# Both products of an encoder's MLP by one level of Strassen's algorithm, in its form with seven products and shared sums

## The chip, the cores and the metric

The kernel runs on one core of one Trainium2 chip, in one launch. The metric is the device time of one execution in microseconds; the kernel before takes 1821.32 us, the median of three runs (1820.94, 1821.32 and 1827.15). On this scale a difference of 0.5%, some 9 us, is about what a comparison can tell from none.

## The reference

One encoder layer runs over 1024 prompt frames and 64 sample frames, together 1088 tokens, with a width of 1024. Four mixers (a convolution, two kinds of attention, a linear recurrence) and a memory attention come first. The change is in the last part, a squared-ReLU MLP with 4096 inner columns, and the final norm:

```
h = _rmsnorm(x, norm_ffn[l])
return x + jnp.square(jax.nn.relu(h @ w_up[l])) @ w_down[l]      # w_up (1024, 4096), w_down (4096, 1024)
...
y_prompt = _rmsnorm(x, norm_final)
```

All inputs and outputs are fp32. Every product is made to nearly fp32 accuracy out of rounded parts: each operand is split into a high part and a low part, and three matmuls (high by high, high by low, low by high) are added in PSUM.

## The kernel before, in words

Everything is held transposed: the partitions are 128 of the 1024 channels, the columns are tokens. Tokens are in two groups, group 0 with 512 and group 1 with 576, the latter cut into chunks of 320 and 256 columns (`GR`, line 207), since one matmul writes at most one bank of 512 columns. The residual `xT[g][k]` stays in SBUF from the output projection to the end.

`load_w` (line 179) fetches a weight block of 128 output columns into one of two `wr` buffers, and `split` (line 166) makes its two parts: ScalarE copies to the rounded type, VectorE subtracts. `mm3` (line 185) does three matmuls for each of the kt blocks of 128 in the sum. Every matmul carries its own weight load.

The MLP (lines 1181 to 1266) goes through the 4096 inner columns in 8 steps `c` of 512. In each step `up` makes 4 blocks of 128 inner rows, for both groups: 24 matmuls for each chunk, then Relu and Square on ScalarE, and a split into the pair `hid`. Then `down` takes, for each of the 8 output blocks `m`, a weight block of 512 by 128, 12 matmuls for each chunk, and one VectorE addition of the PSUM sum to `xT` (line 1240). In the first step the whole of group 0 comes ahead of group 1, because the norm of group 1 needs the last sums of the memory attention's output projection (`dense_add`, line 1051). In the last step `down` goes chunk by chunk, and after each chunk `finish` transposes it on TensorE, makes the final norm and stores it (lines 1199 to 1224).

`rms_stats` (line 1030) sums the squares of a group over its 8 blocks, lets TensorE add over partitions, and takes the inverse root (`rstd_chain`, line 140); `rms_apply` (line 1040) multiplies and splits.

A planner at build time fixes each engine's order of instructions: it takes what its model holds ready by priority, which is the order of the program unless `tc.cur_priority` says otherwise, and gives out the buffers of a pool as earlier users let go of them. On the chip every engine goes through its list in that order. All large transfers of this part are issued on SP's queue.

## Time and profile before

| | |
|---|---|
| median of three runs | 1821.32 us |
| the profiled execution's own time | 1827.22 us |
| its span in the trace | 1825.5 us |
| granted TensorE clock, mean over the span | 0.988 |
| TensorE (PE) busy | 1766.5 us (97%) |
| VectorE (DVE) busy | 1056.7 us (58%) |
| ScalarE (ACT) busy | 802.6 us (44%) |
| GpSimd (POOL) busy | 98.4 us (5%) |
| moved by DMA | 141.79 MB |

A busy share is an average over stages with different limits: the mixers fill the first 800 us or so, the MLP everything from 1045 us to the end. Matmuls are pipelined and their recorded durations overlap, so the time that one takes up is read from start to start. DVE records overlap a little too.

### The profile page before, as it was taken

What the parts mean: (1) busy time and instruction counts of PE and PEld (TensorE: products, weight loads), DVE (VectorE), ACT (ScalarE), POOL (GpSimd) and SP (SyncE); (2) the same over time, 40 slices, a digit from 0 to 9 for tenths busy, and PEclk for the clock granted to TensorE, in tenths of its full rate; (3) what the DMA queues carried; (4) which work ended last, traced back from release to release, by engine and by line L of the source; (5) the groups of instructions that cost most, each with busy time, mean ns of one, the idle gap of its engine ahead of it and who ended that gap; (6) DMA issues with size and microseconds to landing.
All of it is one profiled execution on the core that took longest, in us unless ns stands there. A gap on an engine that the chain in (4) does not pass through costs nothing. (4 is left out here: it accounts for less than half of the span.)

```text
span 1825.5 us, 29328 instructions
## 1 busy us (share of the span) xinstructions
PE 1766.5 (97%) x11454; PEld 1542.6 (85%) x11467; DVE 1056.7 (58%) x2209; ACT 802.6 (44%) x1691; POOL 98.4 (5%) x199
## 2 busy tenths in 40 slices
PE   7999999999999998999999999999999999999997
PEld 5877767777877886988899999999999999999987
DVE  6455779879887887857768564232323232332335
ACT  6464566455447843546455361413131323232233
POOL 3011202001120200000000000000000000000000
PEclk9999999999999999999999999999999999999999
DMA  8221222222223565422322322111111112111212
GB/s 252 75 73 41 60 53 77 59 80 71 82 77 103 152 179 163 140 87 65 109 76 70 107 73 58 35 52 42 44 44 47 47 36 58 35 52 36 58 41 99
DMA packets 225178, 141.79 MB, mean 78 GB/s; under 512 B 14478, under 2 KB 214607, under 8 KB 225039
## 3 DMA queue, kind: packets, MB, share of 16 engines
q1 hardware_dynamic: 224783, 139.90, 25.8%
q8 instruction: 90, 1.47, 0.3%
q14 instruction: 49, 0.40, 0.1%
q0 software_dynamic: 256, 0.01, 0.0%
HBM read 111.97 MB, written 27.87 MB: 77 GB/s over the span
## 5 line engine op out<-in xcount | busy, mean ns | idle before, releaser
L71 PE MATMUL pu<-ap,wh 128*128 128x512 f32 (+2 forms) x1536 | 363.9, 328 | 0.1
L74 ACT ACTIVATE wh<-wr 128x1024 fp32r<-128x1024 f32 (+1 forms) x196 | 170.2, 868 | 428.5 <-PE pdn L71 285.9
L71 PEld LDWEIGHTS pu<-ap,wh 128*128 128x128 f32 x1536 | 261.7, 189 | 20.7 <-DVE ap L168 0.3
L71 PE MATMUL pu<-ap,wl 128*128 128x320 f32 (+2 forms) x768 | 251.1, 327 | 0.0
L168 DVE TENSOR_TENSOR wl<-wr,wh 128x1024 fp32r<-128x1024 f32 (+1 forms) x196 | 193.3, 986 | 91.8 <-ACT wh L74 85.7
L1240 DVE TENSOR_TENSOR xT<-xT,pdn 128x512 f32<-128x512 f32 (+2 forms) x192 | 102.2, 532 | 202.8 <-PE pdn L71 202.8
L71 PE MATMUL pa<-ap,wh 128*128 128x256 f32 (+2 forms) x768 | 189.2, 335 | 7.8 <-ACT ap L74 6.8
L71 PE MATMUL pm<-hx,wh 128*128 128x512 f32 (+1 forms) x640 | 180.2, 369 | 1.3 <-DVE hx L276 0.8
L71 PE MATMUL pdn<-aq,wh 128*128 128x256 f32 (+1 forms) x896 | 181.2, 295 | 0.0
L71 PE MATMUL pm<-ap,wh 128*128 128x256 f32 (+1 forms) x768 | 165.0, 308 | 0.0
L71 PEld LDWEIGHTS pu<-ap,wl 128*128 128x128 f32 x768 | 145.3, 189 | 10.2
L71 PEld LDWEIGHTS pdn<-aq,wh 128*128 128x128 f32 x896 | 148.4, 189 | 4.4
L71 PEld LDWEIGHTS pa<-ap,wh 128*128 128x128 f32 x768 | 133.7, 194 | 19.1 <-ACT ap L74 7.8
L71 PE MATMUL pdn<-hid,wh 128*128 128x512 f32 x448 | 139.3, 392 | 0.0
L71 PE MATMUL pdn<-aq,wl 128*128 128x320 f32 x448 | 132.6, 296 | 0.0
L71 PEld LDWEIGHTS pm<-hx,wh 128*128 128x128 f32 x640 | 112.1, 194 | 21.2 <-issue 1.7
L71 PE MATMUL pa<-ap,wl 128*128 128x512 f32 (+2 forms) x384 | 128.7, 336 | 1.3 <-DVE wl L168 1.3
L71 PEld LDWEIGHTS pm<-ap,wh 128*128 128x128 f32 x768 | 124.2, 192 | 5.1 <-issue 1.9
L760 DVE SCALAR_TENSOR_TENSOR y<-ext,cwT,y 128x288 f32<-128x288 f32 (+2 forms) x300 | 125.3, 446 | 2.9
L71 PE MATMUL pm<-ap,wl 128*128 128x256 f32 (+1 forms) x384 | 114.3, 298 | 0.0
L71 PE MATMUL pm<-hx,wl 128*128 128x512 f32 (+1 forms) x320 | 113.4, 354 | 0.0
L74 ACT ACTIVATE rl<-pu 128x320 f32<-128x320 f32 (+2 forms) x96 | 44.8, 467 | 150.4 <-PE pu L71 150.4
(335 smaller groups left out, 3120.2 us busy)
## 6 DMA issues: line engine op xcount, KB each, us to landing
wr<-in_w_up_dram SPq DMA_DIRECT2D x36, 512.0 KB
wr<-in_w_down_dram SPq DMA_DIRECT2D x64, 256.0 KB
wr<-in_w_in_dram SPq DMA_DIRECT2D x24, 512.0 KB
wr<-in_w_out_dram SPq DMA_DIRECT2D x16, 512.0 KB
wr<-in_w_mq_dram SPq DMA_DIRECT2D x16, 512.0 KB
wr<-in_w_mo_dram SPq DMA_DIRECT2D x32, 256.0 KB
xt<-in_x_prompt_dram SPq DMA_DIRECT2D x8, 512.0 KB
wr<-in_w_mk_dram SPq DMA_DIRECT2D x8, 512.0 KB
```

The lines of the kernel that those rows point to most:

```text
L71: nc.tensor.matmul(out, lhsT=lhsT, rhs=rhs, start=start, stop=stop, **kw)
L74: nc.scalar.activation(out=out, in_=in_, func=func, **kw)
L168: V.tensor_tensor(out=lo, in0=src, in1=hi.bitcast(F32), op=ALU.subtract)
L760: V.scalar_tensor_tensor(out=y[:, :n], in0=ext[:, j:j + n], scalar=cwT[:, ct, j:j + 1], in1=y[:, :n], op0=ALU.mult, op1=ALU.add)
L1240: V.tensor_tensor(out=xs, in0=xs, in1=ps[:, :cn], op=ALU.add)
```

## The change

Both products are cut into two by two blocks. For the product up, a unit is a pair of adjacent blocks of 128 output rows; the other cut halves the sum (channels 0 to 511 and 512 to 1023), and the third cut takes the token groups as halves, 512 and 576, where the shorter one counts as padded with zeros. A unit has 7 products in place of 8: B11, B21 and T4 with 512 columns, T1, T2, B22 and T3 with 576, each with half the sum (`mul`, 12 matmuls for each piece). The 576 columns go as pieces of 288 into two banks (`mul2`). The operands are sums: T1 to T4 of the normed inputs are built and split once ahead of the loop; sums of the weight blocks (`sums`, four additions of 512 columns) and five splits (`wform`) are made for each of the 16 units. Products are added partly in PSUM and partly by VectorE (`plus`), with one shared intermediate `t1`. Relu and Square come after the sums. Then GpSimd forms the T1 to T4 of the inner activations, and seven stores for each unit write them to `hid_d` in DRAM. The residual is stored to `x2_d` as the memory attention's second half finishes it, and loaded again ahead of the product down.

The product down has 8 steps `c`, each reading 14 tiles of `hid_d` and splitting them (`hidden`; for T3 and T4 the subtraction is on GpSimd), and for each of 4 pairs `j` of output blocks 7 products with 6 matmuls for each piece, 7 weight splits of 256 columns, four weight sums on GpSimd, and the additions to `xT`. The shared term is gathered in `a1[j]` by GpSimd. In the last step two of the seven products are done after the others, by token chunks, so that `finish` can follow each. The old code for the MLP (lines 1181 to 1266) is gone; its `finish` returns nearly unchanged.

```
+    x2_d = dram.tile([KD, P, T], F32, name="x2_d")
+    hid_d = dram.tile([DFF // (2 * P), 7, P, 576], F32, name="hid_d")
...
+    UB = {"ap": 16, "aq": 12, "xt": 20}
+    up_ = ctx.enter_context(tc.tile_pool(name="up", bufs=16))
+    pools.append(up_)
+    def unit(tag, dt=F32):
+        return up_.tile([P, 576], dt, name=tag, tag=tag, bufs=UB[tag])
+    xT = [[unit("xt")[:, :n] for k in range(KD)] for g, (t0, n, _) in enumerate(GR)]
...
+            rstd_chain(up_, cn, ps[:, :cn], [("xt", UB["xt"])] * 3, scale=1.0 / D, out=rr[:, c0:c0 + cn])
...
+    def normed(g, k, gains, rr, c0, cn):
+        hf = unit("xt")
+        V.scalar_tensor_tensor(out=hf[:, :cn], in0=xT[g][k][:, c0:c0 + cn], scalar=gains[:, k:k + 1],
+                               in1=rr[:, c0:c0 + cn], op0=ALU.mult, op1=ALU.mult)
+        return hf
...
+            if store:
+                nc.sync.dma_start(out=x2_d[m][:, t0:t0 + n], in_=xT[g][m])
...
+                rr0, h3 = rr, rms_apply(0, g_ffn, rr, 0)
+            dense_add(g, w_mo, HALF * P, KD - HALF, om[HALF:], ps1, store=True)
...
+    N1, N2, HN = 512, 576, 288
+    NU = DFF // (2 * P)
+    B11, T1, B21, T2, B22, T3, T4 = range(7)
+    WIDTH = {B11: N1, B21: N1, T4: N1, T1: N2, T2: N2, B22: N2, T3: N2}
...
+    def bank():
+        return psm.tile([P, 512], F32, name="pw", tag="w", bufs=2)
+    def banks():
+        return psm.tile([P, 2, 512], F32, name="pz", tag="z", bufs=3)
...
+    def mul(ps, w, b, start, cols):
+        for k, (bh, bl) in enumerate(b):
+            last = k == len(b) - 1
+            mm(ps, w[0][:, k], bh[:, cols], start and k == 0, False, skip_group_check=not start)
+            mm(ps, w[0][:, k], bl[:, cols], False, False, skip_group_check=not start)
+            mm(ps, w[1][:, k], bh[:, cols], False, last, skip_group_check=not start)
+    def mul2(ps, w, b, start, n=N2):
+        mul(ps[:, 0, :HN], w, b, start, slice(0, HN))
+        mul(ps[:, 1, :n - HN], w, b, start, slice(HN, n))
+    def split_pool(hi, lo, src):
+        act(hi, src, AF.Copy)
+        Q.tensor_tensor(out=lo, in0=src, in1=hi.bitcast(F32), op=ALU.subtract)
...
+    t1s = [fz.tile([P, N2], F32, name=f"t1_{i}", bufs=1) for i in range(2)]
+    for t in t1s:
+        Q.memset(t[:, N1:], 0.0)
+    rr1 = rms_stats(1, psm, "w")
+    late = [lambda: fz.tile([P, N2], F32R, name="fz", tag="fz")] * 12
+    late = [lambda: unit("aq", F32R)] * 12 + late
+    hb = {B11: h3[:4], B21: h3[4:]}
+    for f in (T2, T1, B22):
+        hb[f] = [[late.pop(0)() for _ in range(2)] for k in range(4)]
+    for f in (T3, T4):
+        hb[f] = [[unit("xt", F32R) for _ in range(2)] for k in range(4)]
+    for k in range(4):
+        h12 = normed(1, k, g_ffn, rr1, 0, N2)
+        h11 = normed(0, k, g_ffn, rr0, 0, N1)
+        V.tensor_tensor(out=h11[:, :N1], in0=h12[:, :N1], in1=h11[:, :N1], op=ALU.subtract)
+        act(h11[:, N1:], h12[:, N1:], AF.Copy)
+        h22 = normed(1, k + 4, g_ffn, rr1, 0, N2)
+        t2 = unit("xt")
+        V.tensor_tensor(out=t2, in0=h22, in1=h11, op=ALU.subtract)
+        split(*hb[T2][k], t2)
+        split(*hb[T1][k], h11)
+        split(*hb[B22][k], h22)
+        Q.tensor_tensor(out=h12, in0=h22, in1=h12, op=ALU.subtract)
+        split_pool(*hb[T3][k], h12)
+        h21 = normed(0, k + 4, g_ffn, rr0, 0, N1)
+        Q.tensor_tensor(out=h21[:, :N1], in0=h21[:, :N1], in1=t2[:, :N1], op=ALU.subtract)
+        split_pool(hb[T4][k][0][:, :N1], hb[T4][k][1][:, :N1], h21[:, :N1])
...
+    def wform(src):
+        pr = [unit("ap", F32R)[:, :4 * P].rearrange("p (k c) -> p k c", k=4) for _ in range(2)]
+        split(*pr, src)
+        return pr
+    def sums(a11, a12, a21, a22, s1, eng):
+        eng.tensor_tensor(out=s1, in0=a21, in1=a22, op=ALU.add)
+        eng.tensor_tensor(out=a21, in0=a11, in1=a21, op=ALU.subtract)
+        eng.tensor_tensor(out=a11, in0=s1, in1=a11, op=ALU.subtract)
+        eng.tensor_tensor(out=a12, in0=a12, in1=a11, op=ALU.subtract)
+    def square(c):
+        act(c, c, AF.Relu)
+        act(c, c, AF.Square)
+    def plus(out, a, b, eng=V):
+        eng.tensor_tensor(out=out, in0=a, in1=b, op=ALU.add)
+    for i in range(NU):
+        r1 = fetch_w(w_up, 0, KD, 2 * i * P)
+        r2 = fetch_w(w_up, 0, KD, (2 * i + 1) * P)
+        wh, wl = (wp.tile([P, KD, P], F32R, name=nm, tag=nm) for nm in ("wh", "wl"))
+        split(wh, wl, r1)
+        s1 = unit("ap")[:, :4 * P].rearrange("p (k c) -> p k c", k=4)
+        sums(r1[:, :4], r1[:, 4:], r2[:, :4], r2[:, 4:], s1, V)
+        S2, S1, S4, S3, A22 = (wform(r) for r in (r1[:, :4], s1, r1[:, 4:], r2[:, :4], r2[:, 4:]))
+        t1 = t1s[i % 2]
+        W, Z, X = bank(), banks(), banks()
+        mul(W, (wh[:, :4], wl[:, :4]), hb[B11], True, slice(0, N1))
+        act(t1[:, :N1], W, AF.Copy)
+        mul2(Z, S2, hb[T2], True)
+        c12 = unit("ap")
+        plus(halves(c12), halves(t1), Z[:, :, :HN])
+        mul2(X, S1, hb[T1], True)
+        c22 = unit("ap")
+        plus(halves(c22), halves(t1), X[:, :, :HN])
+        mul(W, (wh[:, 4:], wl[:, 4:]), hb[B21], False, slice(0, N1))
+        c11 = unit("ap")
+        act(c11[:, :N1], W, AF.Relu)
+        act(c11[:, :N1], c11[:, :N1], AF.Square)
+        mul2(X, S4, hb[B22], False)
+        plus(halves(c12), halves(c12), X[:, :, :HN])
+        square(c12)
+        mul2(Z, S3, hb[T3], False)
+        plus(halves(c22), halves(c22), Z[:, :, :HN])
+        square(c22)
+        mul2(Z, A22, hb[T4], False, N1)
+        c21 = unit("ap")
+        plus(c21[:, :HN], t1[:, :HN], Z[:, 0, :HN])
+        plus(c21[:, HN:N1], t1[:, HN:N1], Z[:, 1, :N1 - HN])
+        square(c21[:, :N1])
...
+        t3, t2, t4 = (unit("xt") for _ in range(3))
+        Q.tensor_tensor(out=t3, in0=c22, in1=c12, op=ALU.subtract)
+        Q.tensor_tensor(out=c12[:, :N1], in0=c12[:, :N1], in1=c11[:, :N1], op=ALU.subtract)
+        Q.tensor_tensor(out=t2, in0=c22, in1=c12, op=ALU.subtract)
+        Q.tensor_tensor(out=t4[:, :N1], in0=c21[:, :N1], in1=t2[:, :N1], op=ALU.subtract)
+        for f, t in ((B11, c11), (T1, c12), (B21, c21), (T2, t2), (B22, c22), (T3, t3), (T4, t4)):
+            nc.sync.dma_start(out=hid_d[i, f, :, :WIDTH[f]], in_=t[:, :WIDTH[f]])
+    fz_ctx.close()
...
+    places = ([lambda: pools[0].tile([P, 576], F32R, name="ap", tag="ap")] * 16
+              + [lambda: fq.tile([P, 576], F32R, name="fq", tag="fq")] * 6
+              + [lambda: unit("ap", F32R)] * 14 + [lambda: unit("aq", F32R)] * 8)
+    turn = [0]
+    def place():
+        turn[0] += 1
+        return places[(turn[0] - 1) % len(places)]()
...
+    def hidden(c):
+        hb = {}
+        for f in (B11, T1, B21, T2, B22, T3, T4):
+            hb[f] = []
+            n = WIDTH[f]
+            for i in (2 * c, 2 * c + 1):
+                raw = unit("aq")[:, :n]
+                nc.sync.dma_start(out=raw, in_=hid_d[i, f, :, :n])
+                pr = [place()[:, :n] for _ in range(2)]
+                (split_pool if f in (T3, T4) else split)(*pr, raw)
+                hb[f].append(pr)
+        return hb
...
+    def down_w(c, j):
+        raw = wp.tile([P, KD, P], F32, name="wr", tag="wr").rearrange("p (k m) c -> p k m c", m=2)
+        nc.sync.dma_start(out=raw.rearrange("p k m c -> p k (m c)"),
+                          in_=w_down[4 * c * P:4 * (c + 1) * P, 2 * j * P:2 * (j + 1) * P].rearrange(
+                              "(k p) c -> p k c", p=P))
+        raw = raw.rearrange("p (k h) m c -> p h m k c", h=2)
+        return [raw[:, h, m] for m in range(2) for h in range(2)]
...
+    NC = DFF // (4 * P)
+    for c in range(NC):
+        hb = hidden(c)
+        end = c == NC - 1
+        if end:
+            for i in range(2):
+                gf.append(unit("ap"))
+                nc.sync.dma_start(out=gf[i][:, :512], in_=norm_final[i * 512:(i + 1) * 512].partition_broadcast(P))
+        for j in range(NJ):
+            x11, x21 = xT[0][2 * j], xT[0][2 * j + 1]
+            x12, x22 = xT[1][2 * j], xT[1][2 * j + 1]
+            a11, a12, a21, a22 = down_w(c, j)
+            p1, p2 = wpair(), wpair()
+            A11, A12 = form(p1, 0, a11), form(p1, 2, a12)
+            s1 = fs.tile([P, 2, P], F32, name="s1", tag="s1")
+            sums(a11, a12, a21, a22, s1, Q)
+            if not end:
+                S1, S4 = form(p1, 4, s1), form(p2, 4, a12)
+            S2, S3, A22 = form(p2, 0, a11), form(p2, 2, a21), form(p2, 6, a22)
+            W, Z = bank(), banks()
+            mul(W, A11, hb[B11], True, slice(0, N1))
+            if c:
+                tmp = unit("aq")[:, :N1]
+                act(tmp, W, AF.Copy)
+                plus(a1[j], a1[j], tmp, Q)
             else:
+                act(a1[j], W, AF.Copy)
+            if not end:
+                X = banks()
+                mul2(X, S1, hb[T1], True)
+                plus(halves(x22), halves(x22), X[:, :, :HN])
+            mul(W, A12, hb[B21], False, slice(0, N1))
+            plus(x11, x11, W)
+            mul2(Z, S2, hb[T2], True)
+            plus(halves(x12), halves(x12), Z[:, :, :HN])
+            if not end:
+                mul2(X, S4, hb[B22], False)
+                plus(halves(x12), halves(x12), X[:, :, :HN])
+            mul2(Z, S3, hb[T3], False)
+            plus(halves(x22), halves(x22), Z[:, :, :HN])
+            mul2(Z, A22, hb[T4], False, N1)
+            plus(x21[:, :HN], x21[:, :HN], Z[:, 0, :HN])
+            plus(x21[:, HN:], x21[:, HN:], Z[:, 1, :N1 - HN])
+            if end:
+                plus(x21, x21, a1[j])
+                plus(x12[:, :N1], x12[:, :N1], a1[j], Q)
+                plus(x22[:, :N1], x22[:, :N1], a1[j], Q)
+        if end:
+            ws = []
+            for j in range(NJ):
+                a11, a12, a21, a22 = down_w(c, j)
+                p = wpair()
+                s1 = fs.tile([P, 2, P], F32, name="s1", tag="s1")
+                sums(a11, a12, a21, a22, s1, Q)
+                ws.append((form(p, 0, s1), form(p, 2, a12)))
+            finish(0, 0, N1)
+            for c0, cn in GR[1][2]:
+                cols = slice(c0, c0 + cn)
+                for j in range(NJ):
+                    x12, x22 = xT[1][2 * j][:, cols], xT[1][2 * j + 1][:, cols]
+                    W = bank()[:, :cn]
+                    mul(W, ws[j][0], hb[T1], True, cols)
+                    plus(x22, x22, W)
+                    mul(W, ws[j][1], hb[B22], False, cols)
+                    plus(x12, x12, W)
+                finish(1, c0, cn)
```

## Rows read from the trace of the kernel before

**Rows 1.** The page, busy time by engine, and its chain of waits by engine and line.
```profile
PE 1766.5 (97%) x11454; PEld 1542.6 (85%) x11467; DVE 1056.7 (58%) x2209; ACT 802.6 (44%) x1691; POOL 98.4 (5%) x199
...
PE 40%; ACT 0%; DVE 0%; issue 0%; DVEq 0%
```
**Rows 2.** The chain of waits in order of time: start us, us, what.
```profile
1142.07 47.44 PE pu L71 x288
1189.51 47.52 PE pdn L71 x288
```
**Rows 3.** Windows: stretch and length; PE, PEld, DVE, ACT, POOL busy; PEclk; DMA share; GB/s.
```profile
300.00:600.00 300.00, 289.32 (x2058) 234.89 (x2068) 251.34 (x564) 162.10 (x369) 32.55 (x45) 0.97 0.27 79
900.00:1000.00 100.00, 99.37 (x714) 94.39 (x714) 71.51 (x176) 55.88 (x139) 0.00 (x0) 1.00 0.27 81
...
0.00:90.00 90.00, 77.20 (x475) 63.07 (x476) 52.83 (x122) 50.59 (x116) 21.50 (x74) 1.00 0.55 164
```
**Rows 4.** Timeline of PE in the MLP: start us, us, instruction; three matmuls for each pair.
```profile
1071.45 0.46 PE L71 MATMUL pu<-ap,wh 128*128 128x320 f32 x2
...
1071.89 0.40 PE L71 MATMUL pu<-ap,wh 128*128 128x256 f32 x2
...
1072.25 0.40 PE L71 MATMUL pu<-ap,wh 128*128 128x256 f32 x2
```
**Rows 5.** Timeline of DVE as the MLP begins.
```profile
1053.55 1.22 DVE L168 TENSOR_TENSOR wl<-wr,wh 128x1024 fp32r<-128x1024 f32 x1
1054.69 0.42 DVE L149 TENSOR_TENSOR rst<-rr 128x256 f32<-128x256 f32 x1
1055.02 0.49 DVE L168 TENSOR_TENSOR ap<-hf,ap 128x320 fp32r<-128x320 f32 x1
...
1056.16 0.42 DVE L151 SCALAR_TENSOR_TENSOR rr<-rst,rr 128x256 f32<-128x256 f32 x1
1056.50 1.01 DVE L1046 SCALAR_TENSOR_TENSOR hf<-xT,g_ffn,rr 128x320 f32<-128x320 f32 x2
1057.42 0.69 DVE L168 TENSOR_TENSOR hid<-rl,hid 128x512 fp32r<-128x512 f32 x1
1058.02 0.49 DVE L168 TENSOR_TENSOR ap<-hf,ap 128x320 fp32r<-128x320 f32 x1
```
**Rows 6.** Groups on DVE and ACT: line, shapes, count; busy us, mean ns; idle before.
```profile
L1240 DVE TENSOR_TENSOR xT<-xT,pdn 128x512 f32<-128x512 f32 x64 | 44.0, 688 | 84.1 <-PE pdn L71 84.1
L1218 DVE SCALAR_TENSOR_TENSOR aqw<-pft,rsy,gf 128x512 f32<-128x512 f32 x16 | 11.3, 747 | 0.5
...
L74 ACT ACTIVATE aqw<-xT 128x576 f32<-128x576 f32 x8 | 5.4, 675 | 0.0
```
**Rows 7.** Timeline of POOL in the mixers.
```profile
135.33 0.59 POOL L866 TENSOR_TENSOR ky<-hx,hk 128x192 f32<-128x192 f32 x1
...
155.03 1.01 POOL L913 TENSOR_TENSOR hqe<-hq,heb 128x384 f32<-128x384 f32 x1 [5.96 <-ACT heb L74]
```
**Rows 8.** Timelines of POOL and of DVE where both run.
```profile
451.45 0.68 POOL L865 TENSOR_TENSOR qz<-hx,hq 64x192 f32<-64x192 f32 x1 [123.04 <-ACT hx L74]
452.21 1.45 POOL L866 TENSOR_TENSOR ky<-hx,hk 128x192 f32<-128x192 f32 x1
...
451.58 1.63 DVE L168 TENSOR_TENSOR wl<-wr,wh 128x1024 fp32r<-128x1024 f32 x1
...
526.45 1.02 POOL L865 TENSOR_TENSOR qz<-hx,hq 64x192 f32<-64x192 f32 x1
...
526.94 0.47 DVE L436 TENSOR_TENSOR vT<-pm,rb 128x320 f32<-128x320 f32 x1
```
**Rows 9.** Timeline of PE, the first matmuls of the product up.
```profile
1045.29 0.63 PE L71 MATMUL pu<-ap,wh 128*128 128x512 f32 x2
```
**Rows 10.** The chain of waits, its end.
```profile
1805.32 8.27 PE pdn L71 x69
...
1820.08 0.66 DVEq L1297
```

More of the change, by code (lines that the diff above doesn't have):

```diff
@@ L1004 @@
     mx.close()
[L1005 to L1011 removed]
+    UB = {"ap": 16, "aq": 12, "xt": 20}
[4 more added lines that the diff above has]
+    xT = [[unit("xt")[:, :n] for k in range(KD)] for g, (t0, n, _) in enumerate(GR)]
     def pair2():
[L1014 removed]
+        return [unit("aq", F32R) for _ in range(2)]
     def wide():
[L1017 removed]
+        return unit("aq")
     def sumsq(g):
@@ new lines @@
+    fz_ctx.close()
+    wq = ctx.enter_context(tc.tile_pool(name="wq", bufs=2))
+    fq = ctx.enter_context(tc.tile_pool(name="fq", bufs=6))
+    fs = ctx.enter_context(tc.tile_pool(name="fs", bufs=2))
+    NJ = KD // 2
+    xT = [[unit("xt")[:, :n] for k in range(KD)] for g, (t0, n, _) in enumerate(GR)]
+    for j in range(NJ):
+        for k in (2 * j, 2 * j + 1):
+            for g, (t0, n, _) in enumerate(GR):
+                nc.sync.dma_start(out=xT[g][k], in_=x2_d[k][:, t0:t0 + n])
+    a1 = [unit("xt")[:, :N1] for j in range(NJ)]
@@ new lines, in wpair, with form, finish @@
+    def wpair():
+        count[0] += 1
+        return [(wp, wq)[count[0] % 2].tile([P, KD, P], F32R, name=nm, tag=nm) for nm in ("wh", "wl")]
+    def form(dst, slot, src, n=2):
+        pr = [t[:, slot:slot + n] for t in dst]
+        split(*pr, src)
+        return pr
+    def finish(g, c0, n):
+        for i in range(0, n, P):
+            w = min(P, n - i)
+            t = GR[g][0] + c0 + i
+            np_ = max(0, min(w, SP - t))
+            ss = fs.tile([P, 2], F32, name="fss", tag="fss")
+            ps = banks()
+            yt = [unit("aq") for _ in range(2)]
+            for kb in range(2):
+                for k in range(4):
+                    nc.tensor.transpose(ps[:w, kb, k * P:(k + 1) * P], xT[g][4 * kb + k][:, c0 + i:c0 + i + w], ident)
+                act(yt[kb][:w, :512], ps[:w, kb], AF.Square, accum_out=ss[:w, kb:kb + 1])
+            V.tensor_tensor(out=ss[:w, 0:1], in0=ss[:w, 0:1], in1=ss[:w, 1:2], op=ALU.add)
+            r = rstd_chain(fs, 1, ss[:w, 0:1], "rf", scale=1.0 / D, parts=w)
+            for kb in range(2):
+                V.scalar_tensor_tensor(out=yt[kb][:w, :512], in0=ps[:w, kb], scalar=r, in1=gf[kb][:w, :512],
+                                       op0=ALU.mult, op1=ALU.mult)
+                ys = slice(kb * 512, (kb + 1) * 512)
+                if np_:
+                    nc.sync.dma_start(out=y_p[t:t + np_, ys], in_=yt[kb][:np_, :512])
+                if np_ < w:
+                    nc.sync.dma_start(out=y_s[t + np_ - SP:t + w - SP, ys], in_=yt[kb][np_:w, :512])
@@ new lines @@
+    NC = DFF // (4 * P)
[23 more added lines that the diff above has]
+                plus(a1[j], a1[j], tmp, Q)
+            else:
+                act(a1[j], W, AF.Copy)
[30 more added lines that the diff above has]
+                cols = slice(c0, c0 + cn)
+                for j in range(NJ):
+                    x12, x22 = xT[1][2 * j][:, cols], xT[1][2 * j + 1][:, cols]
[5 more added lines that the diff above has]
+                finish(1, c0, cn)
```

113 lines of the change are left out of this document (16 added, 97 removed).

## The prediction

> **What bounds the kernel now.** I read the busy times first, then the chain of waits, then windows and timelines of the MLP. TensorE is busy 97% of the span, and the part of the chain that the profile follows, 40%, is all TensorE [rows 1]. In order of time it is pieces of 288 matmuls: 47.44 us for a step of the product up, 47.52 us for a step of the product down, one behind the other without a gap [rows 2]. So in the MLP only TensorE's time counts. From start to start, three matmuls of 320 columns take 0.44 us and three of 256 take 0.36 us [rows 4], 0.1467 and 0.120 us each. A step up has 96 of each kind, so one of 512 takes 47.44/96 - 0.1467 - 0.120 = 0.2275 us. The three fit a line, columns/2.4 GHz plus 13 to 14 ns; the clock was at the upper of its two levels (PEclk 1.00 [rows 3]). I take 0.1337 us for 288 columns and 0.107 us for 224.
>
> **TensorE's work.** Up, a unit after has 24 matmuls of 512, 4 x 24 + 12 = 108 of 288 and 12 of 224: 24 x 0.2275 + 108 x 0.1337 + 12 x 0.107 = 21.18 us, for 16 units 338.9 us. Before: 8 x 47.44 = 379.5 us. Down, one (c, j) is half of a unit, 10.59 us, 32 of them 338.9 us (the chunked end of the last step comes to the same within 0.1 us); before 8 x 47.52 = 380.2 us. The number of matmuls stays 2304 for each product; only columns go, 4352 to 3840. **Gain: 40.6 + 41.3 = 81.9 us.** Should a matmul of 224 take no less than one of 256, 5 us of it are lost. Everything else is what the new form costs, and nearly all of it is whether the other engines keep up.
>
> **Prices of the other engines.** DVE from start to start: 1.14 us for 1024 columns, 0.60 for 512, 0.40 for 320, 0.33 for 256 [rows 5]; so 0.67 for 576 (estimate from that line). The form with a third operand (SCALAR_TENSOR_TENSOR) takes 0.46 for 320 [rows 5], thus 0.67 and 0.74 for 512 and 576. An addition from PSUM costs as much (688 ns recorded [rows 6], against 0.69 for the split [rows 5]). ACT: 0.675 us for 576 [rows 6]. POOL: 0.59 us for 192, 1.01 for 384 [rows 7], a slope of 2.2 ns a column: 0.73, 1.29 and 1.43 us for 256, 512 and 576.
> POOL and DVE also hinder each other. A POOL product of 192 columns took 1.45 us instead of 0.59 while DVE ran a split of 1024, and that split, begun at 451.58 while an earlier POOL product ran to 452.13, took 1.63 us instead of 1.22 [rows 5, 8]. Each excess is about what was left of the other's instruction. A DVE product with one input in PSUM was not touched: 0.47 us for 320 beside a running POOL [rows 8]. So I let DVE's instructions with two SBUF inputs (splits, weight sums, norms) and POOL's exclude each other, and additions from PSUM run free.
> The Trainium skill (SBUF — State Buffer, "Who interferes with whom") says the same as a rule: the two share a read port, and whoever has it blocks the other for its whole instruction. The trace agrees here (1.45 against 0.59 us). Without that rule the stall of the product down, below, would be about 3 us, with it about 19; by its worst order it is the second rival.
>
> **Losses, part by part.**
> (a) Into the MLP. Before, TensorE goes from the last output projection to the first `pu` at 1045.29 [rows 9] without a gap, since group 0 has 4 x 24 matmuls of 512, 21.8 us, that don't need group 1's norm. That norm is complete at 1056.5 [rows 5], 11 us later. After, only the products with B11 and B21 don't need it, and two units' shared tiles allow 48 matmuls of 512, 10.9 us. Then T1, T2, B22 need, for each k of 4 in turn, four norms (2 x 0.67 + 2 x 0.74), two differences (0.60 + 0.67) and three splits (3 x 0.67): 6.1 us of DVE, 24.4 us in all, to 35.4 us. Partial sums over the first three k of three products are 7.2 us more of cover (0.75 x 9.6). Loss 35.4 - 18.1 = 17.3 us if POOL disturbs nothing. POOL's 16 instructions here (8 x 1.43 + 8 x 1.29 = 21.8 us) exclude DVE's; all in the way, it is 39 us. If the buffers let T2 run far ahead, 10. I take 25, nearer to the undisturbed end, as POOL's part for each k comes after most of DVE's. T3 and T4 are then some 10 us later than T2; the products of two units that don't need them take 6 us, so a few microseconds of the 25 are theirs, and a lower clock on resuming is in them too.
> (b) Units up. DVE has 1.14 + 9 x 0.60 with two SBUF inputs and 4 x 0.67 + 0.67 from PSUM, 9.9 us of 21.2; POOL 5.4 us; ACT 14 instructions of at most 0.675 us [rows 6] and one of 1024 columns, under 11 us: no engine binds. A wait is added: the last product adds into the banks that DVE must first have read (`c22`), 0.67 us and a signal. Queued behind it on TensorE is the next unit; the planner can put that unit's first product (2.7 us) ahead. None of it showing: 0; all: 16 us. In a window with DVE at 72% TensorE lost 0.6% [rows 3]; I take 5. On SP seven stores stand ahead of the next fetches; these have a unit's time. 48 MB in 339 us, and in the product down as much, are 142 to 150 GB/s, less than the 164 GB/s which took 0.55 of the DMA engines in the first 90 us [rows 3].
> (c) Between the products. Reading the first 14 inner tiles (3.9 MB) and x (4.5 MB) at 298 GB/s (164 over its share of 0.55 [rows 3], an estimate) takes 28 us if all is exposed; but the first tiles' buffers come free 12 to 15 us ahead of the end of the product up, and x is wanted pair by pair. What is left is the first weight forms, whose buffers lie where B22 was: I take 4 (0 to 28).
> (d) Down, for (c, j): DVE has 7 x 0.33 (weight splits) and a quarter of a step's ten inner splits (4 x 0.60 + 6 x 0.67, so 1.6), 3.9 us with two SBUF inputs, and from PSUM 0.60 + 4 x 0.67 + 0.37 + 0.30 = 3.95 us: 7.9 of 10.6 us. POOL has 4 x 0.73 (weight sums), 1.29 (`a1`) and a quarter of 2 x 1.43 + 2 x 1.29: 5.6 us. Each of POOL's six instructions delays DVE between not at all and wholly: DVE is at 7.9 to 13.5 us. About a third of each, since half of DVE's work is free of it: near 9.8 us, 92%. TensorE lost 0.6% with DVE at 72%, 3.6% with DVE at 84% (289.3 of 300) [rows 3]. Lower end 2 us, upper 28 x 2.9 = 81. I extend the two windows to 5.6% of 339, 19 us.
> (e) The last step. POOL also adds `a1` twice (2.58 us): 6.8 us for each j, where TensorE has 7.4, and four more weight sums (11.7 us) before the chunks' end. In `finish`, 9 blocks of nine instructions on DVE (two of 0.747 us [rows 6]) now stand beside a tail of 13 us of matmuls instead of 47. Before, 6.5 us follow the last matmul of the MLP (1813.6 to 1820.1 [rows 10]). Between 3 and 25 more; I take 9.
> The stores of x ahead of the MLP and the renamed buffers: TensorE is not waiting for DMA there, 0 (-3 to 3).
> **Sum:** -81.9 + 25 + 5 + 4 + 19 + 9 = -20 us. The profiled execution took 1827.2 us, 5.9 us over the median, without a gap in the MLP that would explain it; I take the difference to the median: 1821.3 - 20 = **1801 us**.
>
> **Rivals.**
> Clean: the planner fills every wait, POOL and DVE rarely meet. Losses 17 + 2 + 0 + 2 + 4 = 25, minus 57 us: 1764. For it: DVE at 72% cost TensorE 0.6%; against: no window of before has POOL and DVE both this busy.
> DVE and POOL bind the product down (slower): with their exclusion in a bad order a (c, j) takes 13 us instead of 10.6: 67 us over 28, and with 25 + 5 + 4 + 9 = 43 it is +28: 1849. It decides from (81.9 - 43)/28 = 1.4 us of stall for each (c, j), a period of 12.0 us. For it the doubled POOL times [rows 8]; against it that half of DVE's work reads PSUM.
> The changes of stage eat it: all of POOL's work in the way at the beginning (39) and half of the reload exposed (14), with 5 + 19 + 9: 86, +4: 1825, no change. For it: nothing covers TensorE there once 18 us are used; against: inner tiles lie ready long before.
> That the work on TensorE doesn't shrink needs a floor of 0.14 us for a matmul; the 0.120 us of 256 columns speaks against.
>
> **Chances.** Forecast 0.42 (its own range 1782 to 1820), clean 0.20, binding DVE and POOL 0.20, stage changes 0.18. A difference under 0.5% (1812 to 1830) can't be told from no change. Faster: 0.20 + most of the forecast (0.32) + 0.04 of the stage changes = 0.56. Same: 0.09 + 0.10 = 0.19. Slower: 0.19 + 0.01 + 0.04 and the rest, 0.25. The range reaches past the clean case and to the binding one: 1758 to 1850.
>
> **What would show it.** Right: 288-column matmuls at 0.134 us from start to start; a gap of TensorE of 15 to 30 us about 1056 to 1090; units up within 22 us; periods of (c, j) of 11 to 11.5 us with DVE above 85% and POOL's 512-column additions well over 1.29 us; the end of the span some 9 us later behind the last step's start than the work asks. Wrong: DVE below 80% and no waits in the product down (clean), a period above 12 us (binding), or stores and loads of the inner tiles late on TensorE's path.

## The result: 2009.9 us, 10% slower

After: 2009.87 us, median of 4 runs (2003.20 to 2017.72); before, beside it: 1823.26 us (1820.94 to 1827.15). The ratio is 1.102, 95% interval 1.098 to 1.107. The forecast was 1801 us, range 1758 to 1850: wrong in sign, and far outside the range. Where a run below has the time of one execution only, its second one was slow, at a granted clock of 0.65 to 0.74. The profiled execution of after has a span of 2001.5 us, before's 1825.5: 176 us to explain.

The page of after, with the lines that answer to [rows 1]; the lower ones are busy tenths and the granted clock in 40 slices.

```profile
PE 1771.6 (89%) x11454; PEld 1537.8 (77%) x11467; DVE 1373.5 (69%) x2621; ACT 903.6 (45%) x1919; POOL 432.3 (22%) x493
...
PE   7999999999999768999997488988888899998876
...
PEclk9999999999999978999999699988889899999988
```

TensorE has the same 11454 matmuls with 82 us less of columns, and is busy 5 us more. Its clock is why: the granted clock was 0.939 over the span against 0.988 before, and 0.90 in the product up, where it stands still besides. In the two following views of after (windows, columns as in [rows 3]: the entry, the product up from its third unit, the product down; then what TensorE waited for in the second stretch: us, times, longest) this is to be seen.

```profile
1074.00:1127.00 53.00, 22.96 (x72) 14.82 (x73) 43.55 (x54) 19.36 (x35) 20.89 (x14) 0.71 0.09 26
1172.00:1546.00 374.00, 330.97 (x2004) 305.10 (x2004) 183.77 (x229) 137.09 (x219) 83.06 (x56) 0.90 0.36 122
1612.00:1925.00 313.00, 281.59 (x1763) 255.64 (x1761) 238.18 (x400) 116.57 (x272) 144.10 (x143) 0.95 0.36 119
```
```profile
PE pz L71 <- ACT ap L74: 27.2, 14, 2.0
PE pw L71 <- ACT t L74: 14.6, 14, 1.1
PE pz L71 <- DVE ap L1279: 1.7, 2, 0.9
```

Two waits in each of 14 units, 1.0 and 1.9 us: 43.5 us of idle time with the two of 1.7 us in all, and about as much again in matmuls at a clock under 1.00.

Stage by stage, from the first copy of each product on ACT and the last matmul of each stage. A stage's loss is its time less TensorE's own time at the forecast's 21.18 us a unit, 10.59 us a (c, j) (7.4 in the last step, with 12.8 us of products behind it) and 6.5 us of end; a first copy comes one product behind the start of its unit (2.7 us) or of its (c, j) (1.4 us):

| stage of after | time, us | TensorE's own | loss | forecast (bounds) |
|---|---|---|---|---|
| ahead of the MLP: last projection ends at 1073.6, before at 1045.3 | | | 28 | 0 (-3 to 3) |
| (a) to the third unit's first copy, 1172.1 | 98.5 | 45.1 | 53 | 25 (10 to 39) |
| (b) units 3 to 16, to 1546.0 | 373.9 | 293.8 | 80 | 5 (0 to 16) |
| (c) to the second step's first copy, 1612.2 | 66.2 | 43.7 | 22 | 4 (0 to 28) |
| (d) to the last step's first copy, 1925.7 | 313.5 | 254.2 | 59 | 19 (2 to 81) |
| (e) to the end of the chain, 1996.1 | 70.4 | 47.5 | 23 | 9 (3 to 25) |

Together 266 us; less the 81.9 us of work, and less 8.6 us by which the MLP of before was over its own work (768.3 us for 759.7; 1.8 us of it in the first step, 6.8 in the last), that is 176 us, the difference of the spans. So the list of terms was complete but for one taken at nothing. Three terms lie outside their bounds: the stretch ahead of the MLP, (a) and (b), together 131 of the 204 us by which the losses exceed the forecast's 62; (b) alone is 75.

### The profile page after: what moved, and what is told of

Read it like the earlier page. It is cut to its first block, busy times and chain, and to the rows that moved or that the text cites. A ratio compares the mean times of both kernels' runs of the same rounds, so it can differ in the third digit from the quotient of the medians.

```text
span 2001.5 us, 31035 instructions
## 1 busy us (share of the span) xinstructions
PE 1771.6 (89%) x11454; PEld 1537.8 (77%) x11467; DVE 1373.5 (69%) x2621; ACT 903.6 (45%) x1919; POOL 432.3 (22%) x493
## 4 chain that ended last, share of the span: by engine, by line
PE 40%; DVE 14%; issue 4%; ACT 3%; POOL 3%; DMA 2%; SPq 0%; POOLq 0%; DVEq 0%; ACTq 0%
PE pz L71 19%; PE pa L71 8%; PE pq L71 4%; PE pw L71 4%; DVE wl L168 4%; DVE xt L1279 2%; DMA aq<-hid_d 1%; PE pmo L71 1%; DVE wr L1270 1%; PE pms L71 1%; DVE wr L1271 1%; DVE ap L168 1%; ACT wh L74 1%; ACT aq L74 1%; DVE y L762 1%
## 5 line engine op out<-in xcount | busy, mean ns | idle before, releaser
L74 ACT ACTIVATE wh<-wr 128x256 fp32r<-128x256 f32 (+2 forms) x312 | 182.6, 614 | 372.6 <-PE pz L71 109.1
L168 DVE TENSOR_TENSOR wl<-wr,wh 128x256 fp32r<-128x256 f32 (+2 forms) x312 | 242.7, 799 | 53.6 <-ACT wh L74 51.7
L71 PE MATMUL pz<-ap,wh 128*128 128x288 f32 (+1 forms) x848 | 180.9, 303 | 28.1 <-DVE xt L1279 15.4
L71 PEld LDWEIGHTS pz<-ap,wh 128*128 128x128 f32 x848 | 143.1, 195 | 40.8 <-DVE xt L1279 15.3
L71 PE MATMUL pw<-ap,wh 128*128 128x512 f32 (+2 forms) x464 | 154.5, 409 | 21.8 <-ACT t L74 16.0
L71 PE MATMUL pz<-aq,ap 128*128 128x288 f32 x576 | 119.0, 370 | 45.1 <-ACT ap L74 33.0
L1279 DVE TENSOR_TENSOR xt<-xt,pz 128x576 f32<-128x576 f32 (+2 forms) x184 | 113.3, 632 | 63.9 <-PE pz L71 63.0
L71 PEld LDWEIGHTS pz<-aq,ap 128*128 128x128 f32 x576 | 109.7, 255 | 57.7 <-ACT ap L74 39.3
L71 PE MATMUL pz<-ap,wl 128*128 128x288 f32 (+1 forms) x424 | 127.2, 300 | 0.1
L71 PEld LDWEIGHTS pw<-ap,wh 128*128 128x128 f32 x464 | 86.0, 199 | 40.4 <-ACT t L74 22.8
```

What stands on the lines that cost most here:

```text
L71: nc.tensor.matmul(out, lhsT=lhsT, rhs=rhs, start=start, stop=stop, **kw)
L74: nc.scalar.activation(out=out, in_=in_, func=func, **kw)
L168: V.tensor_tensor(out=lo, in0=src, in1=hi.bitcast(F32), op=ALU.subtract)
L1279: eng.tensor_tensor(out=out, in0=a, in1=b, op=ALU.add)
```

## The experiments

### Ahead of the MLP: where x lies, and whom it shares a ring with

A ring, here, is the tiles of one tag of a pool. `x_tiles_apart` gives three pools in the place of one:

```diff
-    up_ = ctx.enter_context(tc.tile_pool(name="up", bufs=16))
+    ups = {t: ctx.enter_context(tc.tile_pool(name="u" + t, bufs=UB[t])) for t in ("ap", "xt", "aq")}
```

> Only the memory of the 'xt', 'ap' and 'aq' tiles changes: three pools in the order ap, xt, aq instead of one pool, so that x lies where the kernel before had it; sizes and counts stay. Theory: the 28 us lost ahead of the MLP come from where the x tiles lie (their loads wait for memory that the last work of the mixing lanes still holds). Then the first load of x is issued near 676 us instead of 719 us, the last output projection ends near 1045 us instead of 1073 us, and the whole is about 1980 us. Rival: the loads are late because of the order of work around them (queue, planner), not of the place; then the projection's end stays within 3 us of 1073 us and the whole near 2010 us.

Measured: 1996.99 us; the projection ends at 1065.1 us. Both expectations missed. The loads of x, on SP's queue in the timelines of after and of this run (start us, us, instruction):

```profile
718.89 0.80 SPq L1143 DMA_DIRECT2D xt<-xT_d  x2
...
755.26 8.63 SPq L1143 DMA_DIRECT2D xt<-xT_d  x4
```
```profile
675.18 2.71 SPq L1143 DMA_DIRECT2D xt<-xT_d  x6
...
752.84 7.54 SPq L1143 DMA_DIRECT2D xt<-xT_d  x8
```

The first half comes 44 us sooner, so the place was a cause. The second half stays late: in the trace its tiles are asked for behind the temporaries of the first group's norm, which since the change take tiles of the same tag `xt`. So `x_own_ring` (with the norm in place, below) parts these:

```diff
-    UB = {"ap": 16, "aq": 12, "xt": 20}
+    UB = {"ap": 16, "xt": 16, "aq": 12, "xw": 4}
...
-        rr = unit("xt")
+        rr = unit("xw")
```

> On top of the norm in place: x has a ring of 16 tiles of its own at its old address, the temporaries of the norms another ring of 4. Theory: the loads of x's second half were late in the run with x apart because x shared its ring with the temporaries of the norm, and tiles of one ring are handed out in the order of the trace; with rings of their own the loads stand in the queue where they stood in the kernel before. Then the projections give back all of the 28 us: last output projection near 1045 us, whole near 1973 us (norm in place alone 2001). Rival: ring or no ring, x comes late because the memory or the order of norms and additions on DVE changed; then the projection ends at 1060 us or later, as with x apart (-4 to -9 us).

Measured: 1972.10 us, 29 us below the run with the norm in place alone; all 16 loads are issued from 676.7 to 698 us, as before; the projection ends at 1051.0 us. 23 of the 28 us are back. The remaining 5 us are within what this end differs by among the later profiles, in which this stage is the same (1047.4 to 1055.2 us).

### Units up: the order of the trace

`weights_early` moves one call:

```diff
-    for i in range(NU):
+    def prep(i):
         r1 = fetch_w(w_up, 0, KD, 2 * i * P)
...
         act(c11[:, :N1], c11[:, :N1], AF.Square)
+        if i + 1 < NU:
+            nxt = prep(i + 1)
```

> Only the order of the trace changes in the product up: the fetch, sums and splits of the next unit's weights stand behind c11 of the unit at work instead of behind its last result. Theory: a unit takes 26.8 us instead of 21.2 because DVE's stream has the weight sums of the next unit behind c21, whose product ends the unit, so TensorE waits for sums and splits at each unit's begin and then runs at the lower clock for a while. Then the units fall to 21.3 to 22.5 us, the 16 units give back 65 to 75 us, and the whole is 1935 to 1950 us. Rival: the sums are slow because POOL's four operations of the unit hold the memory port that DVE needs; these are all still there, so a unit stays above 25 us and the whole above 1980 us.

Measured: 1920.95 us, ratio 1.051 (1.043 to 1.059), 89 us below after, more than expected; units of 21.1 to 21.2 us (one first copy at 1278.43, the next at 1299.58). In after (timelines of DVE and POOL, then of TensorE, then one line of DVE in the middle of the next unit; the bracket is the idle time ahead and its releaser):

```profile
1296.45 0.76 DVE L1279 TENSOR_TENSOR ap<-ap,pz 128x576 f32<-128x576 f32 x1 [2.30 <-PE pz L71]
1300.52 0.75 DVE L1279 TENSOR_TENSOR ap<-t,pz 128x288 f32<-128x288 f32 x2 [3.32 <-PE pz L71]
1301.19 0.87 DVE L1269 TENSOR_TENSOR ap<-wr 128x512 f32<-128x512 f32 x1
1302.09 1.78 DVE L1270 TENSOR_TENSOR wr<-wr 128x512 f32<-128x512 f32 x1
1303.90 1.65 DVE L1271 TENSOR_TENSOR wr<-ap,wr 128x512 f32<-128x512 f32 x1
...
1301.59 1.73 POOL L1318 TENSOR_TENSOR xt<-ap 128x576 f32<-128x576 f32 x1
1303.39 1.61 POOL L1319 TENSOR_TENSOR xt<-ap,xt 128x512 f32<-128x512 f32 x1
...
1303.14 0.72 PE L71 MATMUL pw<-ap,wh 128*128 128x512 f32 x2 [1.04 <-ACT t L74]
...
1306.26 0.85 PE L71 MATMUL pz<-aq,ap 128*128 128x288 f32 x2 [1.93 <-ACT ap L74]
1307.76 4.50 PE L71 MATMUL pz<-aq,ap 128*128 128x288 f32 x19
...
1313.53 1.23 DVE L168 TENSOR_TENSOR wl<-wr,wh 128x1024 fp32r<-128x1024 f32 x1
```

DVE stands idle for 3.3 us, reads the unit's last product (c21), and only then makes the next unit's weight sums. Its raw weights were there: the split of one of the two raw blocks, which needs no tile of the ring `ap`, is made in the middle of the unit (1313.53, for the unit whose first product begins at 1323.4). The sums, which ask `ap` for a tile behind c21, are not. That points to the ring; the run below moves the place in the program and the turn in the ring together, and does not part them. TensorE begins the next unit's first product (B11) ahead of the last one, then waits for ACT's copy of it (1.0 us, ahead of B21) and for the form S2 (1.9 us, ahead of T2). The sums also fall together with POOL's four operations, which stretch two of them from 0.69 to 1.78 and 1.65 us. Behind the wait a matmul of 288 columns takes 4.50/19 = 0.24 us instead of 0.134: the lower of the two levels of the clock, 1.2 GHz. In `weights_early` the same sums stand in the middle of the unit; its window from the third unit on, and the timeline:

```profile
1172.00:1465.00 293.00, 291.98 (x1991) 277.27 (x1989) 158.67 (x220) 131.45 (x214) 84.44 (x56) 1.00 0.45 156
```
```profile
1261.27 0.75 DVE L1279 TENSOR_TENSOR ap<-t,pz 128x576 f32<-128x576 f32 x1 [2.33 <-PE pz L71]
1261.94 0.68 DVE L1269 TENSOR_TENSOR ap<-wr 128x512 f32<-128x512 f32 x1
1262.66 0.69 DVE L1270 TENSOR_TENSOR wr<-wr 128x512 f32<-128x512 f32 x1
1263.39 0.69 DVE L1271 TENSOR_TENSOR wr<-ap,wr 128x512 f32<-128x512 f32 x1
```

POOL's work is unchanged; it now meets additions from PSUM and the split of 1024 columns (2.09 and 2.24 us in two units, instead of 1.23), for which TensorE does not wait. The rival (POOL itself) falls, and the forecast's 21.18 us of work for a unit stands.

### The entry: tiles, port, and DVE's own row

`norm_in_place` writes the norm over x and so needs no temporary tiles (T1 is split ahead of T2 with it):

```diff
-        hf = unit("xt")
+        hf = xF[g][k] if inplace else unit("xt")
```

> Only the forms of the normalised x change their tiles: the norm is written over x (which is in DRAM by then), so the four temporary tiles per k go, and T3 and T4 get their tiles inside the loop. Theory: the entry into the MLP takes some 53 us too long because only four tiles are left for temporaries, so that DVE's norms for the next k wait for POOL and ACT to finish T3 and T4 of this k (about 12 us for each k). Then a k costs 6 to 8 us, the inner units start 15 to 20 us sooner and the whole is about 1992 us. Rival: it is the sum of the work of DVE and POOL, which exclude each other, that takes 12 us for a k; then less than 6 us come back and the whole stays above 2004 us.

Measured: 2001.29 us; loss (a) falls from 53 to 45 us: between the two expectations. DVE no longer waits for tiles that POOL holds, as it did in after (first line); what is left is that its instructions and POOL's stretch each other (timeline of this run, then of `entry_on_dve`):

```profile
1098.49 1.48 DVE L1048 SCALAR_TENSOR_TENSOR xt<-xt,g_ffn 128x512 f32<-128x512 f32 x2 [1.42 <-POOL xt L1231]
```
```profile
1108.38 1.96 DVE L168 TENSOR_TENSOR aq<-xt,aq 128x576 fp32r<-128x576 f32 x1
1110.26 1.82 DVE L1253 TENSOR_TENSOR xt<-xt 128x576 f32<-128x576 f32 x1
1112.01 1.96 DVE L168 TENSOR_TENSOR fz<-xt,fz 128x576 fp32r<-128x576 f32 x1
...
1107.81 1.92 POOL L1257 TENSOR_TENSOR xt<-xt 128x576 f32<-128x576 f32 x1
1109.69 3.66 POOL L1232 TENSOR_TENSOR xt<-xt 128x512 fp32r<-128x512 f32 x2
```
```profile
1093.88 0.76 DVE L168 TENSOR_TENSOR aq<-xt,aq 128x576 fp32r<-128x576 f32 x1
1094.54 0.75 DVE L168 TENSOR_TENSOR fz<-xt,fz 128x576 fp32r<-128x576 f32 x1
1095.21 0.76 DVE L168 TENSOR_TENSOR aq<-xt,aq 128x576 fp32r<-128x576 f32 x1
```

`entry_on_dve`, on top of it, with a second loop for T3 and T4:

```diff
-        Q.tensor_tensor(out=h12, in0=h22, in1=h12, op=ALU.subtract)
-        split_pool(*hb[T3][k], h12)
+        V.tensor_tensor(out=h12, in0=h22, in1=h12, op=ALU.subtract)
+        split(*hb[T3][k], h12)
```

> On top of the norm in place: T3 and T4 of the normalised x are made in a second loop and by DVE; POOL has nothing at the entry. Theory (shared port): in the run with the norm in place DVE's splits took 1.75 to 1.96 us instead of 0.67 beside POOL's operations of 1.8 us; without POOL, T1, T2 and B22 are ready 19 us after the norm's sum (near 1107 us), T3 and T4 10 to 11 us later, and the third unit's copy of its first product comes at 1145 to 1155 us instead of 1167 us; whole about 1985 to 1990 us. Rival: DVE's 28 to 30 us of work are the limit whoever does T3 and T4; the copy stays at 1160 us or later.

Measured: 1995.65 us; the third unit's copy at 1157.5 us, 2 us later than expected, loss (a) 37 us. The splits are back at 0.75 us. What is left is a row of DVE without gaps (31.9 of 32 us). So the entry had both: of 53 us, 16 came from tiles and from POOL beside DVE, and 37 stay, 5 of them because the units are still 26 to 27 us long here.

### The product down: raw tiles and port

`raw_ring` takes the split pairs out of the raw tiles' ring; `down_without_pool` moves POOL's work there to DVE:

```diff
-              + [lambda: unit("ap", F32R)] * 14 + [lambda: unit("aq", F32R)] * 8)
+              + [lambda: unit("ap", F32R)] * 14)
```
```diff
-                (split_pool if f in (T3, T4) else split)(*pr, raw)
+                split(*pr, raw)
...
-            sums(a11, a12, a21, a22, s1, Q)
+            sums(a11, a12, a21, a22, s1, V)
...
-                plus(a1[j], a1[j], tmp, Q)
+                plus(a1[j], a1[j], tmp)
```

> Only the list of places for the split inner tiles changes: the 8 tiles of the tag 'aq' are left to the raw tiles as they come from DRAM (12 instead of about 4 for these), and the split pairs keep 36 tiles instead of 44. Theory: a step of the product down takes 52 us instead of 42.4 because the raw inner tiles of the next step find no free tile, so that their loads are issued late and all of them land, are split and are waited for at the boundary of steps. Then a step falls to 45 to 47 us (four periods of 11.2 us and little between) and the whole to 1965 to 1980 us. Rival: the boundary is long because 14 pairs have to be split by DVE, ACT and POOL beside the weights; fewer places for pairs then make it the same or longer, 50 to 56 us for a step, whole 1995 to 2040 us.

> Only the product down: the weight sums, the addition into a1 and the splits of T3 and T4 move from POOL to DVE; POOL has nothing there. Theory (shared port): what holds DVE up at the steps' boundaries, and the 0.65 us above the ideal in each (c, j), is POOL's part; DVE's own sum is 7.9 + 4 x 0.33 + 0.6 + 0.64 = 10.4 us of 10.6 for a (c, j), so a step falls from 52 to 43 to 46 us, the whole by 40 to 60 us, to 1945 to 1965 us. Rival: DVE then has all of its time taken and is the bound itself: a (c, j) 11.5 us or more and steps of 48 to 52 us, whole 1980 to 2010 us.

Measured: 1999.42 and 1967.17 us, one execution each. A step, from first copy to first copy over six steps, takes in after 52.2 us, raw tiles free 51.5, no POOL 48.6, both (`raw_without_pool`, below) 45.3; TensorE's own is 42.4. Freeing the raw tiles alone did nothing, as its rival had it; without POOL a step was longer than expected (43 to 46), in its rival's range (48 to 52), but the period inside it was TensorE's own (10.6 us, where the rival had 11.5 or more); the two together give 6.9 us. Each cure alone leaves the other cause in the way: without POOL, ACT still waits for the landing of inner tiles (25 us in after, 32 us without POOL, in the two largest groups of its waits for them). Groups by shape in after, and in `raw_without_pool`:

```profile
L168 DVE TENSOR_TENSOR wl<-wr,wh 128x256 fp32r<-128x256 f32 x138 | 77.7, 600 | 1.2 <-ACT wh L74 0.4
L1279 DVE TENSOR_TENSOR xt<-xt,pz 128x576 f32<-128x576 f32 x92 | 68.7, 747 | 23.5 <-PE pz L71 22.7
```
```profile
L1283 DVE TENSOR_TENSOR xt<-xt,pz 128x576 f32<-128x576 f32 x96 | 71.6, 746 | 0.8 <-PE pz L71 0.4
L168 DVE TENSOR_TENSOR wl<-wr,wh 128x256 fp32r<-128x256 f32 x145 | 55.8, 416 | 0.5 <-ACT wh L74 0.5
```

Beside POOL the weight split (two inputs in SBUF) takes 600 ns instead of 416; the addition with an input in PSUM takes 747 and 746. This is the exclusion of [rows 8] in the new kernel. The Trainium skill (SBUF — State Buffer, "Who interferes with whom") has just this division, two SBUF inputs against at most one, and the runs agree with it.

### All together

`all_four` joins `x_own_ring`, `weights_early`, `entry_on_dve` and `down_without_pool`; `raw_without_pool` adds `raw_ring`.

> The four edits together: x in a ring of its own (-28 us), weights of the next unit early (-80 us), the entry without POOL (-15 to -20 us), the product down without POOL (-40 us by the theory of the shared port, 0 if DVE binds). If the losses add up stage by stage, the whole is 2010 - 28 - 80 - 18 - 40 = about 1844 us (1825 to 1890), still not below the kernel before. Rival: what is won in one stage is lost in another (later loads, a clock that stays low), and it is above 1900 us.

Measured: 1840.89 us (1.008, 1.003 to 1.013); forecast 1844. The losses add up by stage: the stretch ahead of the MLP gives back 24 us, the entry 20, the units 81, the product down 35 (expected 28, 18, 80 and 40). Its units, in the window of the product up: TensorE stands still for 1 us in 295.

```profile
1126.00:1421.00 295.00, 293.93 (x2005) 279.24 (x2004) 160.90 (x223) 131.57 (x214) 85.97 (x55) 1.00 0.45 156
```

> All four edits together, and now all 12 'aq' tiles for the raw inner tiles (36 places for split pairs instead of 44). Theory: with POOL away the periods inside a step of the product down are at TensorE's own 10.6 us, and what is left, 6.5 us at each boundary of steps, is the late raw tiles (in the run with the down product without POOL the waits at the boundary end with their landing); then a step falls from 48.8 to 43 to 46 us and the whole from 1841 to 1805 to 1825 us. Rival: the boundary is DVE's 14 splits, which can't be made ahead with fewer places; then a step stays at 48 us or more and the whole at 1838 us or more.

Measured: 1826.77 us, ratio 0.9997 (0.9986 to 1.0008): no difference from before; the step fell as expected, to 45.3 us, the whole lies 2 us above the range. TensorE's busy time is 1711.5 us, 55 less than before; it now stands still for what it saved. By the stages of the table above its losses are 5 us ahead of the MLP, 33 in (a), none in (b), 13 in (c), 18 in (d) and 22 in (e): 89 us, against a gain of 81.9 and the 8.6 of before. The product down's window, and what TensorE waited for in it:

```profile
1477.00:1749.00 272.00, 261.31 (x1742) 242.12 (x1741) 254.36 (x538) 114.94 (x269) 0.00 (x0) 1.00 0.41 137
```
```profile
PE pz L71 <- DVE xt L1283: 10.1, 13, 1.5
```

DVE is busy for 94%, and TensorE's waits there are all for its additions.

### An order that undid the cure, and what else was tried

`t1_first` makes T1 first and gives a unit its products in the order T1, B22, T2, T3, T4; `t1_first_raw10` differs in the places. Both ask for the next unit's weights ahead of c12:

```diff
         if i + 1 < NU:
             nxt = prep(i + 1)
         mul2(X, S4, hb[B22], False)
+        c12 = unit("ap")
+        plus(halves(c12), halves(t1), X[:, :, :HN])
+        mul2(Z, S2, hb[T2], True)
```

> On top of the run before: the forms of the normalised x are made in the order T1, B22, T2, T3, T4, and a unit takes its products in that order, so that TensorE has work as soon as T1 (which needs two of the four norms of a k) is there; and x is read again pair by pair behind the first inner tiles instead of ahead of them. Theory: the entry is a row of DVE work of 30 us, of which TensorE must see the first part early; the third unit begins 10 to 18 us sooner (its copy at 1111 to 1119 us instead of 1129 us), and the DMA share of 0.95 in the 20 us between the products falls, 3 to 8 us more. Whole 1785 to 1808 us if the raw tiles do their part, else 1820 to 1830 us. Rival: two units' slots limit what TensorE may take up before all forms are there; the third unit's copy stays above 1122 us, and the whole within 8 us of the run before.

> As the run before, with 10 'aq' tiles for raw inner tiles and 40 places for split pairs (the last two of 'ap' among them). Theory: the raw tiles need only cover the 3 to 4 us of a load, so 10 do as well as 12 and four more places let DVE split one pair more ahead: 0 to 10 us faster than with 12. Rival: what counts is only the number of raw tiles in flight; then 0 to 10 us slower.

Measured: 1890.96 and 1888.91 us; the 2 us between them tell nothing on the number of raw tiles. The entry gained 9 us (10 to 18 expected); the units went from 21.2 back to 25.9 us. ACT and DVE in `t1_first`, and what TensorE waited for in the product up:

```profile
1329.08 1.06 ACT L74 ACTIVATE wh<-wr 128x1024 fp32r<-128x1024 f32 x1 [3.65 <-DMA wr<-in_w_up_dram]
...
1330.17 1.23 DVE L168 TENSOR_TENSOR wl<-wr,wh 128x1024 fp32r<-128x1024 f32 x1 [4.26 <-ACT wh L74]
1331.31 0.75 DVE L1286 TENSOR_TENSOR ap<-t,pz 128x576 f32<-128x576 f32 x1
```
```profile
PE pz L71 <- DVE ap L1286: 35.1, 12, 4.4
```

An addition that frees TensorE's banks stands on DVE behind a split that waits, by way of ACT, for weights. `t1_first_c12_first` moves the two lines of `prep` behind c12's first addition, `additions_ahead` also the loop of T3 and T4 behind it, and `weights_ahead` that loop behind the second unit's weights.

> As the run with T1 first, and the next unit's weights are asked for behind c12's first addition instead of ahead of it. Theory: in that run a unit took 25.9 us because c12 takes a tile of the ring 'ap' that was promised to the next unit's weight forms, and those wait for this unit's later products; asked for in the other order, units fall back to 21.1 to 21.3 us, the entry stays as it was there (third unit's copy near 1119 us), and the whole is 1815 to 1822 us. Rival: the product order itself costs it (the next product of a unit then follows the addition that frees its banks at once); units stay above 24 us, whole above 1865 us.

> As the run before, and T3 and T4 of the normalised x stand in the trace behind the first unit's c22 and c12, so that their first additions no longer queue behind T3 and T4 on DVE (5.8 us of TensorE's idle time at the entry, and the lower clock behind it). Theory: 4 to 8 us less than the run before, whole 1808 to 1817 us, faster than the kernel before by 0.5 to 1%. Rival: T3 and T4 come as much later as the additions come sooner; within 3 us of the run before.

> As the run before, but the second unit's weights stand ahead of T3 and T4, so that its first three products can fill TensorE while T3 and T4 are made. Theory: 0 to 5 us less than the run before (two units in flight). Rival: the first unit's S3 waits for T3, holds the tiles that the second unit's forms need, and it is 0 to 6 us more.

Measured: 1830.73, 1828.05 and 1828.14 us. Units are back at 21.2 us in the first: the second time that only the place in the trace at which a ring's tiles are asked for decides 5 us a unit. But the entry's gain went with it: counted to the fifth unit's copy the entry loses 34 us in `all_four`, 31.5 in the first two and 27 in `weights_ahead`. The first lies 9 us above its range. The second is 2.7 us below the first, as its rival had it (within 3 us), not by the theory (4 to 8). The third equals the second: the 4.5 us that its entry saves don't show in the whole, and in its profile the projection ahead of the MLP ends at 1055.2 us instead of 1047.4, which no run explains. `last_step_kept` and `last_step_kept_weights_ahead` keep the last step's weight forms instead of loading and summing again:

```diff
             if not end:
                 S1, S4 = form(p1, 4, s1), form(p2, 4, a12)
+            else:
+                p = [place()[:, :4 * P].rearrange("p (k c) -> p k c", k=4) for _ in range(2)]
+                ws.append((form(p, 0, s1), form(p, 2, a12)))
```

> As the run with the additions ahead; in the last step the forms S1 and S4 are made from the step's own weight sums and kept (two tiles for each j) instead of loading the weights again and making the sums a second time, so 16 weight sums (16 x 0.33 = 5.3 us of DVE) and four loads go. Theory: DVE is what the last step waits for (busy over 90% there), so 4 to 8 us go; whole 1818 to 1824 us, at most 0.5% below the kernel before. Rival: the chain of final norms, block after block, is what the end waits for; within 2 us of the run before.

> The same on the run with the second unit's weights ahead: the same 4 to 8 us by the theory, whole 1818 to 1824 us; the two entries differ by less than 3 us, as they did without it.

Measured: 1825.38 us (0.9996, 0.9983 to 1.0010) and 1823.62 us (0.9991, 0.9975 to 1.0007). The first lies 2.7 us, the second 4.5 us under its base, too little to tell the theory from its rival. The traces tell more: from the last step's first copy to the end of the span, 75.1 and 75.2 us became 73.5 in both, 1.7 us, as the rival has it (within 2 us), though DVE is busy 5 us less in this stretch (59.8 us instead of 64.9). A window of the last step in `additions_ahead`, and in `last_step_kept`:

```profile
1749.00:1797.00 48.00, 41.12 (x261) 36.19 (x261) 47.38 (x111) 16.47 (x46) 0.00 (x0) 1.00 0.20 65
```
```profile
1749.00:1797.00 48.00, 42.65 (x273) 37.56 (x274) 43.65 (x104) 17.91 (x51) 0.00 (x0) 1.00 0.10 34
```

So DVE was busy for 99% of the first window, and yet 5 us less of its work shortened the stage by 1.7 us only.

No version is measurably faster than the kernel before. What divides the last step's 21 to 23 us between DVE's additions and the chain of the final norms stays open.

## Why the prediction was wrong

- **TensorE's work, -81.9 us: right.** A unit without waits takes 21.1 to 21.2 us (forecast 21.18), a (c, j) inside a step without POOL 10.5 to 10.6 us (10.59).
- **(b), 5 us (0 to 16), measured 80: the step that failed.** It read "no engine binds" off the sums of busy time, and these were right (DVE 49% in the stretch). It named the wait of the last product on `c22`'s addition; that cost 0.9 us, once, in the last unit, because the planner does begin the next unit's first product ahead, as the forecast said it can. It took for granted that the next unit's weight sums and forms would be made in DVE's free time, and did not ask where in DVE's stream they would stand: behind c21, the last result of the unit. Its bound, all of one addition's wait in each unit, bounded the wrong wait.
- **"Stores of x and the renamed buffers", 0 (-3 to 3), measured 28.** It looked at the added stores and not at what the new pool did: it moved x to other memory and put it into one ring with temporaries. The 28 us arise at 680 to 780 us, 300 us before the edit's own stage.
- **(a), 25 (10 to 39), measured 53.** The row of DVE's work that it summed up is what is left once tiles and POOL are out of the way: 27 to 34 us, with T3 and T4 on DVE too, against its 17.3 undisturbed. POOL's exclusion was bounded by POOL's own 21.8 us; the shortage of tiles, DVE waiting for POOL and POOL for ACT, was left out.
- **(c), (d), (e): 22, 59 and 23 us, inside their bounds, all three taken too low.** For (d) the forecast has the port right (600 ns against 416) and the period inside a step (11.2 us, forecast 11 to 11.5); it took the boundary of steps for free, and that is where 7 of the 10 us a step are. The test it set for itself, DVE above 85%, failed: DVE was at 76% of the stretch, with gaps for TensorE and for raw tiles.
- **The clock.** A lower clock after waits was counted once, within (a). In after it is 37 of the 80 us of (b), what the 43.5 us of idle time leave.
- **Rivals.** "DVE and POOL bind the product down" (1849) and "the stage changes eat it" (1825) both happened in part; none had the product up. Slower had a chance of 0.25.

## What to carry to other kernels

A sum of busy times says that an engine has room; it doesn't say that the planner will use it. Before a wait is priced at nothing, ask where the next iteration's work will stand in the in-order stream of the engine that makes it, and which tiles it must get first: this unit's results and the next one's preparation, in one ring and asked for in the wrong order, cost 80 us here, and one moved call gave it back. Renaming or merging buffers is an edit of every stage that uses them, and is priced at each first use.

## What was not expected of the hardware

- In after TensorE waited 1.0 and 1.9 us in each unit of some 27 us, and ran a part of every unit at its lower level (granted 0.90 over 374 us); in `weights_early`, without these waits, 1.00 was granted over the same units. Idle time (43.5 us) and lower clock (37 us) cost about the same in this stretch.
- Where both POOL and DVE had work queued without a gap, in `norm_in_place`, each pair of 512 or 576 columns took nearly the sum of both: DVE's splits and differences 1.8 to 2.0 us instead of 0.75, POOL's operations 1.8 to 1.9 instead of 1.3 to 1.4. The forecast had the exclusion, at about a third of each instruction in (d).
